# Row tiles of two blocks loaded into idle modulation buffers, and convolution taps kept behind the sums of squares of q and k

## The chip, the cores and the metric

The kernel runs on one core of one Trainium2 chip. The metric is the device time of one execution in microseconds (us). The engines are TensorE (PE, matmuls), VectorE (DVE), ScalarE (ACT), GpSimd (POOL) and SyncE (SP), whose queue issues nearly all DMAs. Each works through its own queue in order.

## The reference, cut to what matters

One layer of a streaming encoder, over 2048 prompt rows and 64 sample rows of width 1024, all in float32:

```python
mod = silu(c) @ w_ada + b_ada                      # six vectors: sh1, sc1, gt1, sh2, sc2, gt2
h = rms_norm(x, norm1_g) * (1 + sc1) + sh1
glu_a, glu_b, q, k, v, g_conv, g_attn = split(h @ w_in)
u = glu_a * sigmoid(glu_b)
conv = silu(layer_norm(depthwise_conv31(u) + b_dw)) @ w_conv_out
q, k = rms_norm(q, q_norm_g), rms_norm(k, k_norm_g)   # per head of 64
o = band_attention(q, k, v, rel_bias) @ w_attn_out
x = x + gt1 * ((sigmoid(g_conv) * conv + sigmoid(g_attn) * o) @ w_o)
h2 = rms_norm(x, norm2_g) * (1 + sc2) + sh2
gate, up = split(h2 @ w_ffn_in)
x = x + gt2 * ((silu(gate) * up) @ w_ffn_out)
```

The change lies in the first half, up to the mixers' outputs; the merge and the feed-forward part are untouched.

## The kernel before

**Blocks and stages.** The 2112 rows are cut into four blocks (`PBLOCKS`, b = 0 to 3; the text calls them blocks one to four): 576 rows, then three times 512. Each block goes through the stages of `ORDER`: q, the first quarter of the convolution channels (0), k, quarter 1, v, quarters 2 and 3, then g, the sixteen column groups of the two gates. Beside these products run the attention of the block, the convolution's taps and its norm, and, during the gates, the norm of the next block's rows. Matmul operands are split into a high and a low part, and each product takes three matmuls. This first half of the kernel ends near 1200 us.

**What sets the order.** The program is written out by Python in one pass. A model of the engines' loads (`Stream`, line 170) decides when the side jobs (`Lane`, line 108) emit their next piece: when PE's modelled time has passed what they yielded. DMA times are not modelled; a load counts as landed a fixed time after it was written (`X_LAG`, 8000 ns of modelled PE time, for row tiles). After that a scheduler lays out each engine's queue, by its own model of the times. It may move an instruction ahead of earlier ones that it believes are not ready. `tc.issue_after(ins)` keeps the instructions of its block behind `ins` on the same engine. Nothing is reordered at run time.

**Rows of the next block.** `load_ahead` (line 1129) takes the next tile of 128 rows from `to_load` and loads it into a buffer with the tag "x" of the pool `wa`, which has three. Stores of v (`store_v`, line 1021) and a few k rows of block one use the same tag. At gate group `NORM_G` (11) of a block, the main loop (line 1616) calls `load_ahead` three times. `norm_tile` (line 1135) then squares the rows on ACT (`square`), takes the power -1/2 of the mean on POOL (`rsqrt_mean`, line 722), scales the rows on DVE, turns them on PE in two groups of four 128x128 pieces (tile `pt`), and makes `hh` and `hl`. With its second group it calls `load_ahead` for one more tile. At most two tiles are in work at a time. `hh` and `hl` are still read by the gates of the block before; `free["columns"]` tells how far they are done with.

**Modulation.** Six products of `c` with `w_ada` are made from slabs of 512 KB (`Slabs`, line 230), which are loaded into four buffers of 4 KB per partition with the tag "wmod". `fill` (line 239) loads the next slab as soon as one is given back. The first sixteen slabs (keys of five parts) are used while block one's rows are prepared; the other 32 are used in blocks two and three, four behind each of the stages 0 to 3 (`MODS`). So the four buffers hold the next four slabs from block one's start to block two's stage 0.

**Taps.** `convolve` (line 1232) applies the 31 taps of a channel quarter, 30 of them one DVE operation each (`y<-u,wd,y`). They are emitted when DVE's modelled load allows, and each stays behind the last score traced so far (`scores`, filled in `softmax_max`, line 1347). In block one's k stage there are no scores yet.

**q and k.** `qk_rows` (line 1032) takes the product of one tile from PSUM: ACT makes squares (`sq`) and a copy (`kn`), DVE sums the squares per head (`ssq<-sq`) and makes the mean (`t<-ssq`), POOL the power (`r<-t,mhalf`), DVE the scaled rows (`kn<-kn,r`), PE turns them (`pt<-ident,kn`), ACT and DVE split them (`part_h`, `part_l`), and SP stores them.

Of the kernel before, what the change touches and what calls it, by code (L numbers as in the profile page):

```python
# [16 lines left out]
P = 128  # L17
# [15 lines left out]
QB = 512  # L33

PBLOCKS = [(0, 576), (576, 1088), (1088, 1600), (1600, 2112)]
# [11 lines left out]
X_LAG = 8000.0  # L47
# [182 lines left out]
class Slabs:  # L230
# [3 lines left out]
    def __init__(self, sync, other, pool, stream, keys, source, held):  # L234
        self.sync, self.other, self.pool, self.stream = sync, other, pool, stream
        self.keys, self.source, self.held = keys, source, held
        self.ready, self.used, self.given, self.freed = [], 0, 0, 0

    def fill(self):
        while len(self.ready) < min(len(self.keys), self.freed + self.held):  # L240
            (src,), a, b = self.source(self.keys[len(self.ready)])
            w = self.pool.tile([P, a, b], F32, tag="wmod", name="wmod", bufs=self.held)
            i = len(self.ready)
            (self.other if i < self.held and i % 2 else self.sync).dma_start(w, src)
            self.ready.append(w)

    def get(self, key):
        assert self.keys[self.used] == key
        self.used += 1
        while len(self.ready) < self.used:  # L250
            self.free(self.freed + 1)
        return self.ready[self.used - 1]

    def done(self):
        self.given += 1
# [356 lines left out]
def streaming_layer(ctx: ExitStack, tc: tile.TileContext, I, O):  # L612
    nc = tc.nc
    stream = Stream()
# [383 lines left out]
            dve.memset(bias[r : r + HD, c : c + HD], BIG)  # L998


    def store_kq(src, n, dst, col, g=None):

        pt = ps_g.tile([P, 4, P], F32, tag="gp", name="pt")
        for hp in range(4):
            pe.transpose(pt[:, hp, :n], src[:n, hp * P : (hp + 1) * P], ident[:n, :n])
        stream.after("act", "pe")
        hi, lo = parts(shape=(P, 4, P))
        if g is None:
            split(hi[:, :, :n], lo[:, :, :n], pt[:, :, :n])
        else:  # L1010
            act.activation(hi[:, :, :n], pt[:, :, :n], AF.Copy, scale=g)
            stream.after("dve", "act")
            dve.scalar_tensor_tensor(lo[:, :, :n], pt[:, :, :n], g, hi[:, :, :n].bitcast(F32), ALU.mult, ALU.subtract)

        def store():
            for j, t in enumerate((hi, lo)):
                nc.sync.dma_start(dst[j, :, :, col : col + n].rearrange("h p t -> p h t"), t[:, :, :n].bitcast(F32))

        stream.at(stream.when("act", "dve"), store)
# [12 lines left out]
    def qk_rows(ps, n, g, dst, col, out_rows, spare=False):  # L1032
        sq = temp("sq", (P, NH, HD))
        ssq = wk.tile([P, NH], F32, tag="ssq8", bufs=5)
        if spare:
            kn = wa.tile([P, 2, NH, HD], F32, tag="x", name="kn", bufs=3)[:, 0]
        else:
            kn = wa.tile([P, NH, HD], F32, tag="kn", bufs=3)
        pv = ps[:n].rearrange("p (h d) -> p h d", h=NH)
        stream.after("act", "pe")  # L1040
        act.activation(sq[:n], pv, AF.Square)
        act.activation(kn[:n], pv, AF.Copy)
        yield stream.when("act")
        dve.tensor_reduce(ssq[:n], sq[:n], AX.X, ALU.add)
        r = rsqrt_mean(wk, ssq[:n], n, NH, HD)
        yield stream.when("pool")
        e, name = either(512, TT_LESS)
        e.tensor_tensor(kn[:n], kn[:n], r.unsqueeze(2).to_broadcast([n, NH, HD]), ALU.mult)
        t = stream.when(name)
        if out_rows is not None:  # L1050
            ko = temp("ko", (P, NH, HD))
            e, name = either(512, TT_LESS)
            e.tensor_tensor(ko[:n], kn[:n], gk[:n].unsqueeze(1).to_broadcast([n, NH, HD]), ALU.mult)
            stream.at(stream.when(name), lambda: nc.sync.dma_start(out_rows, ko[:n].rearrange("p h d -> p (h d)")))
        yield t + KN_LAG
        store_kq(kn.rearrange("p h d -> p (h d)"), n, dst, col, g)
# [70 lines left out]
    ahead_x, to_load = {}, []  # L1127

    def load_ahead():

        if to_load:
            t = to_load.pop(0)
            ahead_x[t] = load_x(t, P, wa, "x", 3), stream.load["pe"] + X_LAG

    def norm_tile(lo, t, free):

        c = slice(t - lo, t - lo + P)
        while t not in ahead_x:
            load_ahead()
        x_t, landed = ahead_x.pop(t)  # L1140
        yield landed
        r = square(x_t, P)
        yield stream.when("pool")
        dve.tensor_scalar(x_t, x_t, r, None, ALU.mult)
        yield stream.when("dve") + PE_LAG
        for g in range(2):
            pt = ps_g.tile([P, 4, P], F32, tag="gp", name="pt")
            h = temp("h32", (P, 4, P))
            for k in range(4):
                pe.transpose(pt[:, k], x_t[:, (4 * g + k) * P : (4 * g + k + 1) * P], ident)  # L1150
            if g:
                stream.at(stream.when("pe"), load_ahead, True)
            stream.after("dve", "pe")
            for k in range(4):
                kk = 4 * g + k
                dve.tensor_scalar(h[:, k], pt[:, k], A1[:, kk, 0:1], B1[:, kk, 0:1], ALU.mult, ALU.add)
            yield stream.when("dve")
            yield lambda: free["columns"] >= c.stop
            f = slice(4 * g, 4 * g + 4)
            act.activation(hh[:, f, c], h, AF.Copy)  # L1160
            yield stream.when("act")
            dve.tensor_tensor(hl[:, f, c], h, hh[:, f, c].bitcast(F32), ALU.subtract)
# [35 lines left out]
    def kts(t, a=0, b=KT):  # L1198
        return [t[:, k] for k in range(a, b)]


    scores = []
    UW = HIST + QB + HIST + SMP
    YW = UW - HIST

# [26 lines left out]
    def convolve(u, y, ct, b):  # L1232
        w = UW if b == 0 else HIST + QB
        n = w - HIST
        states = [(cs_s, HIST + SMP)] if b == 0 else [(cs_p, w)] if b == len(PBLOCKS) - 1 else []
        if states:
            yield stream.when("dve") + TURN_LAG
        for rows_, e in states:
            pt = ps_g.tile([P, 512], F32, tag="gp", name="pt")
            pe.transpose(pt[:HIST, :P], u[:, e - HIST : e], ident)  # L1240
            s = wa.tile([HIST, P], F32, tag="cc", name="cc", bufs=2)
            dve.tensor_scalar(s, pt[:HIST, :P], 0.5, None, ALU.mult)
            stream.at(stream.when("dve"), lambda s=s, rows_=rows_: nc.sync.dma_start(rows_[:, ct * P : (ct + 1) * P], s))
            yield
        gps.tensor_copy(hist[:, ct], u[:, w - HIST : w])
        dve.tensor_scalar(y[:, ct, :n], u[:, :n], wd[:, ct, 0:1], bdw[:, ct : ct + 1], ALU.mult, ALU.add)
        for k in range(1, TAPS):
            with tc.issue_after(scores[-1]) if scores else nullcontext():
                dve.scalar_tensor_tensor(
                    y[:, ct, :n], u[:, k : k + n], wd[:, ct, k : k + 1], y[:, ct, :n], ALU.mult, ALU.add  # L1250
                )
            yield
# [94 lines left out]
    def softmax_max(ps, n, w, bias):  # L1347
        pr = wk.tile([P, 640], F32, tag="pr", name="pr", bufs=8)
        sm = wk.tile([P, 4], F32, tag="sm", name="sm", bufs=9)
        nb = ps.shape[1]  # L1350
        stream.after("dve", "pe")

        dve.tensor_tensor_reduce(
            out=pr[:n, :w].rearrange("p (a b) -> p a b", a=nb), in0=ps, in1=bias.rearrange("p (a b) -> p a b", a=nb),
            scale=-0.125, scalar=3e38, op0=ALU.add, op1=ALU.min, accum_out=sm[:n, 0:1],
        )
        scores.append(dve.last.ins)
        free = stream.when("dve")
        stream.after("act", "dve")
        act.activation(pr[:n, :w], pr[:n, :w], AF.Exp, bias=sm[:n, 0:1], scale=-1.0, accum_out=sm[:n, 2:3])  # L1360
        return pr, sm, free, stream.when("act")
# [230 lines left out]
    for b, stage in ORDER:  # L1592
        lo, hi = PBLOCKS[b]
# [20 lines left out]
        elif stage == "g":  # L1614
            for g in gates(b, free):
                if g == NORM_G:
                    to_load += list(ahead)
                    for _ in range(3):
                        load_ahead()
                    for gen in ahead.values():  # L1620
                        norm_lane.add(gen)
                if g == SIDE_G and b == len(PBLOCKS) - 1:
                    work.drain()
                    conv.drain()
                    stream.flush()
                    side.close()
                    wc = ctx.enter_context(tc.tile_pool(name="wc", bufs=1, side="right"))
                    cs = tile_chunks(*CBLOCKS[0])[0]
                    src = load_mixed(*cs, 0)
                    first_gates = gate_columns(*cs, 0)  # L1630
# [621 lines left out]
```

## Time and profile before

| what | us |
|---|---|
| median of 3 runs | 2994.62 |
| lowest and highest | 2992.54 and 2999.41 |
| the profiled execution | 2994.99 |
| its span, first to last instruction | 2993.2 |
| PE busy in it | 2912.7 |
| DVE busy in it | 2024.7 |
| PE busy in its first 1200 us | 1144.05 |
| PE busy in the other 1793.2 us | 1768.63 |

A row of a timeline gives the start on the span's clock, the length, the engine (a q behind its name means its queue, which issues a DMA), the line, the operation and what it writes and reads, and in brackets how long the engine had been idle and what ended that. Most instructions carry L102, the line of the helper that records them, so they are told apart by their tiles. A row of a table of stretches gives the busy time of each engine in it, the clock that was granted to TensorE (1.00 is full), the mean share of time that the DMA engines worked, and what they moved.

### The profile page before, as it was taken

The numbers are of one execution on the slowest core, as the hardware profiler recorded it, in microseconds if no ns is written. First come the engines' busy times: TensorE is split into PE (matmuls) and PEld (weight loads), VectorE is DVE, ScalarE is ACT, GpSimd is POOL, SyncE is SP. The second block draws the span as 40 slices with busy tenths as digits, with TensorE's granted clock in tenths as the row PEclk, the third lists the DMA queues.
The fourth block names the chain that finished last, engine by engine and source line by source line (L and its number), as shares of the span: only waits on it lengthen the run. The fifth ranks groups of instructions, "written<-read, shape, count | busy, mean of one in ns | idle before, by whom it ended". The sixth has DMA issues, their size and how long they took to land.

```text
span 2993.2 us, 44914 instructions
## 1 busy us (share of the span) xinstructions
PE 2912.7 (97%) x16259; PEld 2593.7 (87%) x16259; DVE 2024.7 (68%) x3596; ACT 1355.1 (45%) x2437; POOL 1141.4 (38%) x734
## 2 busy tenths in 40 slices
PE   7999899999999999989999999999999999999999
PEld 4899777787888788888989889999999999999998
DVE  5887687767857885477677755666666657466666
ACT  3335643662456257464444335534444345344442
POOL 0201310111011102354566433256666741466667
PEclk9999999999999999999999999999999999999999
DMA  8889889888987789885444786423333975333333
GB/s 290 289 284 304 266 288 314 282 255 275 308 280 221 275 246 286 254 293 166 141 141 152 232 269 216 138 89 115 118 101 115 307 248 183 96 93 116 116 102 127
DMA packets 467724, 628.06 MB, mean 210 GB/s; under 512 B 36276, under 2 KB 314664, under 8 KB 467501
## 3 DMA queue, kind: packets, MB, share of 16 engines
q1 hardware_dynamic: 453456, 605.58, 62.5%
q10 hardware_dynamic: 14045, 19.60, 1.9%
q8 instruction: 128, 2.10, 0.3%
q14 instruction: 95, 0.78, 0.1%
HBM read 476.53 MB, written 148.54 MB: 209 GB/s over the span
## 4 chain that ended last, share of the span: by engine, by line
PE 80%; DVE 8%; DMA 4%; ACT 2%; POOL 2%; issue 2%; SPq 1%; ACTq 0%; DVEq 0%; POOLq 0%
PE ps L102 51%; PE pd L102 16%; PE pw L102 5%; DVE y L102 3%; PE sc L102 2%; PE po L102 2%; PE ptp L102 2%; DVE wlo L102 1%; PE pt L102 1%; PE pa L102 1%; ACT whi L102 1%; DMA tg<-g_d 1%; POOL r L102 1%; POOL wlo L102 1%; DVE pw L102 1%
## 5 line engine op out<-in xcount | busy, mean ns | idle before, releaser
L102 PE MATMUL ps<-t,whi 128*128 128x384 f32 (+1 forms) x2112 | 502.5, 322 | 8.8 <-ACT t L102 5.0
L102 POOL TENSOR_TENSOR wlo<-wst,whi 128x1024 fp32r<-128x1024 f32 (+1 forms) x157 | 358.4, 2292 | 287.1 <-ACT whi L102 251.6
L102 ACT ACTIVATE whi<-wst 128x1024 fp32r<-128x1024 f32 (+1 forms) x264 | 257.5, 978 | 331.9 <-PE ps L102 113.8
L102 PE MATMUL ps<-b,whi 128*128 128x384 f32 (+1 forms) x1584 | 381.3, 326 | 6.1 <-DVE early L102 3.3
L102 PEld LDWEIGHTS ps<-t,whi 128*128 128x128 f32 x2112 | 367.7, 188 | 15.8 <-ACT t L102 5.2
L102 DVE SCALAR_TENSOR_TENSOR y<-u,wd,y 128x512 f32<-128x512 f32 (+1 forms) x480 | 369.1, 773 | 6.8
L102 PE MATMUL ps<-hh,whi 128*128 128x512 f32 (+2 forms) x992 | 361.5, 364 | 0.0
L102 DVE TENSOR_TENSOR acc<-acc,pd 128x512 f32<-128x512 f32 (+1 forms) x464 | 311.6, 685 | 66.9 <-PE pd L102 64.1
L102 PE MATMUL ps<-hl,whi 128*128 128x512 f32 (+2 forms) x992 | 345.3, 348 | 0.0
L102 PE MATMUL ps<-hh,wlo 128*128 128x512 f32 (+2 forms) x992 | 345.1, 348 | 0.0
L102 PE MATMUL ps<-t,wlo 128*128 128x384 f32 (+1 forms) x1056 | 339.2, 321 | 0.7 <-POOL wlo L102 0.7
L102 PE MATMUL pd<-whi,hid 128*128 128x512 f32 (+1 forms) x1016 | 325.2, 391 | 0.5 <-DVE acc L102 0.5
L102 PEld LDWEIGHTS ps<-b,whi 128*128 128x128 f32 x1584 | 278.6, 189 | 12.0 <-DVE early L102 4.2
L102 POOL TENSOR_TENSOR r<-t,mhalf 128x1 f32<-128x1 f32 (+3 forms) x68 | 84.1, 1239 | 453.2 <-DVE t L102 448.0
L102 PE MATMUL ps<-b,wlo 128*128 128x384 f32 (+1 forms) x792 | 256.9, 325 | 0.0
L102 ACT ACTIVATE pr<-pr,sm 128x640 f32<-128x640 f32 (+3 forms) x272 | 200.3, 747 | 102.8 <-DVE sm L102 100.5
L102 PEld LDWEIGHTS pd<-whi,hid 128*128 128x128 f32 (+1 forms) x1016 | 185.9, 183 | 45.2 <-DVE acc L102 0.9
L102 PEld LDWEIGHTS ps<-hh,wlo 128*128 128x128 f32 x992 | 186.6, 188 | 21.8
L102 PEld LDWEIGHTS ps<-hh,whi 128*128 128x128 f32 x992 | 187.2, 189 | 18.5 <-issue 1.6
L102 PEld LDWEIGHTS ps<-hl,whi 128*128 128x128 f32 x992 | 187.3, 189 | 15.4 <-issue 1.4
L102 PEld LDWEIGHTS ps<-t,wlo 128*128 128x128 f32 x1056 | 198.2, 188 | 1.9 <-POOL wlo L102 1.3
L102 PE MATMUL pd<-wlo,hid 128*128 128x512 f32 (+1 forms) x508 | 198.5, 391 | 0.0
(225 smaller groups left out, 6173.5 us busy)
## 6 DMA issues: line engine op xcount, KB each, us to landing
whi<-w_din_h SPq DMA_DIRECT2D x72, 512.0 KB, 6.7
wlo<-w_din_l SPq DMA_DIRECT2D x72, 512.0 KB, 7.5
wst<-sum_d SPq DMA_DIRECT2D x132, 256.0 KB, 2.7
wfo<-in_w_ffn_out SPq DMA_DIRECT2D x64, 512.0 KB, 3.3
wmod<-in_w_ada SPq DMA_DIRECT2D x46, 512.0 KB, 7.3
sum_d<-ws SPq DMA_DIRECT2D x88, 256.0 KB, 2.9
wst<-in_w_ffn_in SPq DMA_DIRECT2D x84, 256.0 KB, 3.1
wst<-in_w_in SPq DMA_DIRECT2D x40, 512.0 KB, 9.4
```

What stands on the lines that cost most here:

```text
L102: self.last = f(*args, **kw)
```

## The change

`Slabs` gets a limit `open`: at first only the sixteen slabs of the first modulation may be loaded, and `open_all` lifts it. `norm_tile` calls `open_all` behind the second group of turnings of a block's last tile; for other tiles it calls `load_ahead` as before. `load_ahead` puts the tiles of block three into "x" as before, and those of blocks two and four into "wmod". At `NORM_G` blocks one and three load all four tiles of the next block at once, block two three. The list `scores` becomes `ahead_of_taps`, and the mean that follows each sum of squares of q and k is entered too, so that each tap stays behind the last score or mean traced so far.

```diff
@@ class Slabs
+        self.open = sum(len(key) == 5 for key in keys)
+
     def fill(self):
-        while len(self.ready) < min(len(self.keys), self.freed + self.held):
+        while len(self.ready) < min(self.open, self.freed + self.held):
...
+    def open_all(self):
+        if self.open < len(self.keys):
+            self.open = len(self.keys)
+            self.fill()
@@ qk_rows
         dve.tensor_reduce(ssq[:n], sq[:n], AX.X, ALU.add)
         r = rsqrt_mean(wk, ssq[:n], n, NH, HD)
+        ahead_of_taps.append(dve.last.ins)
@@ load_ahead
             t = to_load.pop(0)
-            ahead_x[t] = load_x(t, P, wa, "x", 3), stream.load["pe"] + X_LAG
+
+            place = ("x", 3) if PBLOCKS[2][0] <= t < PBLOCKS[2][1] else ("wmod", 4)
+            ahead_x[t] = load_x(t, P, wa, *place), stream.load["pe"] + X_LAG
@@ norm_tile
             if g:
-                stream.at(stream.when("pe"), load_ahead, True)
+                stream.at(stream.when("pe"), M.open_all if t + P == lo + QB else load_ahead, True)
@@ convolve
-            with tc.issue_after(scores[-1]) if scores else nullcontext():
+            with tc.issue_after(ahead_of_taps[-1]) if ahead_of_taps else nullcontext():
                 dve.scalar_tensor_tensor(
@@ softmax_max
-        scores.append(dve.last.ins)
+        ahead_of_taps.append(dve.last.ins)
@@ main loop, stage g
                     to_load += list(ahead)
-                    for _ in range(3):
+                    for _ in range(3 if b == 1 else 4):
                         load_ahead()
```

More of the change, by code (lines that the diff above doesn't have):

```diff
@@ L998, in bias_rows @@
             dve.memset(bias[r : r + HD, c : c + HD], BIG)
+    ahead_of_taps = []
     def store_kq(src, n, dst, col, g=None):
@@ L1199, in kts @@
         return [t[:, k] for k in range(a, b)]
-    scores = []
     UW = HIST + QB + HIST + SMP
```

## The prediction

> **What bounds the kernel now.** I read the page of the profile first, for the engine that ends last, then the waits of that engine, then the stretches around its longest waits, engine by engine.
>
> ```profile
> PE 2912.7 (97%) x16259; PEld 2593.7 (87%) x16259; DVE 2024.7 (68%) x3596; ACT 1355.1 (45%) x2437; POOL 1141.4 (38%) x734
> ```
>
> TensorE (PE) is busy for 97% of the span. The change touches no matmul, so all that it can win or lose is idle time of PE, and time in which PE runs at a lower granted clock. The waits of PE (total in us, times, longest) say which idle time is within its reach:
>
> ```profile
> PE pt L102 <- DVE x_t L102: 10.9, 6, 5.7
> PE sc L102 <- DVE sm L102: 7.9, 7, 2.4
> ...
> PE pt L102 <- DVE kn L102: 3.5, 2, 2.3
> ```
>
> Half of the first row is one wait of 5.7 us for a scaled tile of x rows. The third is about rows of q and k. Here is the stretch of the 5.7 us, from the timelines of SyncE's queue (SPq), ScalarE (ACT), GpSimd (POOL), VectorE (DVE) and PE; columns are start, length, what, and in brackets the idle time ahead of it:
>
> ```profile
> 299.12 3.24 SPq L1116 DMA_DIRECT2D x_t<-in_x_prompt  x3
> ...
> 342.98 1.25 SPq L1116 DMA_DIRECT2D x_t<-in_x_prompt  x1
> ...
> 353.33 0.61 ACT L102 ACTIVATE junk<-x_t 128x512 f32<-128x512 f32 x1
> ...
> 343.43 0.55 POOL L102 TENSOR_TENSOR r<-t,mhalf 128x1 f32<-128x1 f32 x1
> ...
> 344.02 0.75 DVE L102 TENSOR_SCALAR x_t<-x_t,r 128x1024 f32<-128x1024 f32 x1 [4.91 <-POOL r L102]
> ...
> 355.90 0.76 DVE L102 TENSOR_SCALAR x_t<-x_t,r 128x1024 f32<-128x1024 f32 x1 [0.23 <-POOL r L102]
> ...
> 356.80 1.09 PE L102 MATMUL pt<-ident,x_t 128*128 128x128 f32 x4 [5.66 <-DVE x_t L102]
> ```
>
> Three tiles of block two's rows are loaded at 299 us, the fourth only at 342.98, when the first has given its buffer back. Its squares start at 353.33, it is scaled at 355.90, and PE, idle since 356.80 - 5.66 = 351.14, turns it at 356.80. The third tile, loaded 43 us earlier, was scaled at 344.02. What the wait does to the clock stands in the table of 4 us stretches (length; busy time of PE, PEld, DVE, ACT, POOL; then granted clock, DMA share, GB/s):
>
> ```profile
> 350.00:354.00 4.00, 1.04 (x5) 0.30 (x3) 1.30 (x6) 3.11 (x9) 0.00 (x0) 0.84 1.07 337
> 354.00:358.00 4.00, 1.09 (x4) 0.72 (x4) 3.08 (x10) 3.29 (x8) 0.56 (x1) 0.50 1.04 356
> 358.00:362.00 4.00, 3.99 (x10) 3.08 (x11) 4.00 (x12) 2.35 (x5) 2.62 (x1) 0.50 0.80 188
> 362.00:366.00 4.00, 4.00 (x22) 3.30 (x21) 4.00 (x9) 1.93 (x4) 0.21 (x1) 0.88 0.29 110
> ...
> 378.00:382.00 4.00, 4.00 (x21) 3.10 (x19) 2.41 (x5) 0.96 (x2) 1.63 (x1) 1.00 1.02 396
> ```
>
> A mean of 0.88 in the fourth row means 0.96 us of it at half clock, so the half clock ends near 362.96; by the first row it began near 352.72.
>
> **The change, part by part.**
>
> *Four row tiles at once.* For blocks two and four the fourth load moves to the other three, at about 302.4 us. The four buffers are idle there, and the extra issue takes SyncE about 1.1 us (3.24 / 3). The fourth tile can then follow the third: its power behind the third's (343.43 + 0.55), its scaling behind the third's (344.77), ready near 346, five us ahead of 351.14. The wait goes: -5.66. With PE busy throughout, I expect the clock to stay up: the 6.16 us from 356.80 to 362.96 at half clock become 3.08. Together **-8.74**. Block four gains nothing: the view of PE's waits has no wait for x_t once block two's rows are turned. The third tile's own short wait stays, since it is for the power on POOL (the 4.91 us on DVE), not for a load.
>
> The Trainium skill ("TensorE: Matmul & The Clock Gate", Terms) prices the penalty as throttled time times (1 - K/N). For 10.24 us at half clock that is an estimate of 5.1 us, and the sum would be 2.0 us better; but the rows show PE idle for the first part of it, and idle time is counted already.
>
> *Modulation slabs later.* The four slabs that fill those buffers now move behind the turning of block two's last tile. What they meet there:
>
> ```profile
> 57.61 4.71 SPq L244 DMA_DIRECT2D wmod<-in_w_ada  x4
> ...
> 363.28 0.49 PE L102 MATMUL pt<-ident,x_t 128*128 128x128 f32 x3
> ...
> 368.70 0.33 SPq L466 DMA_DIRECT2D whi<-w_din_h  x1
> ...
> 381.20 0.47 PE L102 MATMUL ps<-hh,whi 128*128 128x512 f32 x1
> ...
> 388.77 1.93 PE L102 MATMUL pa<-wmod,cl 128*32 128x256 f32 x32
> ...
> wlo<-w_din_l SPq DMA_DIRECT2D x72, 512.0 KB, 7.5
> ```
>
> At 57.61 nothing is gained: PE waits for no DMA between there and block one's k products. Their new place is the second turning of block two's last tile, at 363.28 - 8.74 = 354.5 on the shortened time; they are first read at 388.77 - 8.74 = 380.0. Four slabs are 2.1 MB, 5.3 us at the 396 GB/s of the last stretch above, so even with some microseconds of issue they land near 363, 17 us early. But SyncE issues in order, and behind them stands the second weight of the convolution's first stage: issued at 368.70, used at 381.20, 12.5 us between. Both ends move up alike; 5.3 us of slabs in front leave 7.2, and the page's median from issue to landing is 7.5. I take a loss of **+0.3**. Bounds: 0 (the stretches at 362 to 370 had DMA to spare) and 5.3 with up to 3.1 of lost clock behind it, 8.4.
>
> *Taps behind the sums.* In block one's k stage the rows are:
>
> ```profile
> 103.39 7.04 DVE L102 SCALAR_TENSOR_TENSOR y<-u,wd,y 128x606 f32<-128x606 f32 x8
> 110.34 0.67 DVE L102 TENSOR_REDUCE ssq<-sq 64x8 f32<-64x512 f32 x1
> ...
> 117.14 0.83 DVE L102 SCALAR_TENSOR_TENSOR y<-u,wd,y 128x606 f32<-128x606 f32 x1
> 117.90 0.16 DVE L102 TENSOR_SCALAR t<-ssq 128x8 f32<-128x8 f32 x1
> ...
> 101.95 0.58 ACT L102 ACTIVATE kn<-ps 64x512 f32<-64x512 f32 x1
> 115.48 0.47 ACT L102 ACTIVATE part_h<-pt,gqk 128x256 fp32r<-128x256 f32 x1 [12.95 <-PE pt L102]
> ...
> 118.20 1.65 POOL L102 TENSOR_TENSOR r<-t,mhalf 128x8 f32<-128x8 f32 x1 [4.05 <-DVE t L102]
> ...
> 115.01 0.43 PE L102 MATMUL pt<-ident,kn 64*128 64x64 f32 x4 [2.26 <-DVE kn L102]
> ...
> 120.72 0.63 PE L102 MATMUL pt<-ident,kn 128*128 128x128 f32 x4 [0.94 <-DVE t L102]
> ```
>
> ACT has the squares ready at 102; eight taps keep the sum from DVE until 110.34, and PE waits 2.26 us for the rows at the end. Without them the sum starts near 103.4, 7 us sooner, and this wait goes. The tile behind it has one tap between sum and mean (117.14 to 117.90; the mean is the t row): 0.76 of its 0.94 goes. What the taps lose they take later, beside matmuls. Block three has the same picture:
>
> ```profile
> 711.27 0.59 ACT L102 ACTIVATE kn<-ps 128x512 f32<-128x512 f32 x1
> ...
> 717.25 0.68 DVE L102 TENSOR_REDUCE ssq<-sq 128x8 f32<-128x512 f32 x1
> ...
> 718.81 2.05 POOL L102 TENSOR_TENSOR r<-t,mhalf 128x8 f32<-128x8 f32 x1 [5.89 <-DVE t L102]
> ...
> 721.74 0.63 PE L102 MATMUL pt<-ident,kn 128*128 128x128 f32 x4 [1.23 <-DVE kn L102]
> ```
>
> The sum comes over 5 us after its squares, the wait is 1.23. Together **-2.26 - 0.76 - 1.23 = -4.25**; bounds 0, if the taps stay where they are, and -4.43. One guard is loosened: a tap behind a sum no longer waits for a score traced before it. A tap in front of a score costs up to 0.8 us, seven times at most by the sc row (5.6 in all); I take 0, since a score that is ready still goes first.
>
> Against this part speaks a rule of the Trainium skill ("SBUF — State Buffer", SBUF: two separate sides): a DVE operation with two SBUF inputs and a GpSimd operation lock each other out. The rows fit: the power took 1.65 us with no tap beside it and 2.05 with one. Taps that are freed just as the mean is out would sit beside each power, and the second wait would shrink by 0.36 in place of 0.76, the sum being 0.4 worse.
>
> Sum: -8.74 + 0.3 - 4.25 = -12.7. The profiled execution took 2994.99 us (its span 2993.2 and 1.8 around it), 0.4 above the median of 2994.62. **2994.99 - 12.7 = 2982.3.**
>
> **The rivals.**
>
> *The taps do not move* (they were traced ahead of the sums and keep their place). For it: DVE's order is settled when the program is laid out, not by arrival. Against: in both blocks above the sum came several microseconds behind its squares, so taps passed it that could have waited. 2994.99 - 8.74 + 0.3 = 2986.6.
>
> *More than counted is won.* In block four, v's last weight is late:
>
> ```profile
> 999.68 0.63 SPq L466 DMA_DIRECT2D whi<-w_dqkv_h  x1
> ...
> 1006.83 0.50 PE L102 MATMUL ps<-whi,hh 128*128 128x512 f32 x1 [2.01 <-DMA whi<-w_dqkv_h]
> ```
>
> It is issued behind a store of k rows, which waits for DVE. Sums that come earlier bring that store forward. -2.0 and, by the ratio of the first stall, 1.1 of clock: 2979.2.
>
> *The slabs give the gain back.* The upper bound above, 8.4 for 0.3, makes 2990.4: within 0.2%. For it: DMA is at 1.0 or more from 374 us on. Against: the pocket at 362 to 370.
>
> *Slower: the taps arrive late at the convolution's norm.* In block one a tap behind a sum waits for ACT, which stands from 102.5 to 115.48, so DVE idles where it ran nine taps (7.04 + 0.83 = 7.9 us). From 230 us DVE is full and PE waits at the norm's sums:
>
> ```profile
> 210.00:220.00 10.00, 6.12 (x12) 1.00 0.80 262
> ...
> 260.00:270.00 10.00, 10.00 (x18) 1.00 0.92 308
> ...
> 272.37 0.43 PE L102 MATMUL pm<-s,ones 128*128 128x64 f32 x2 [2.64 <-POOL s L102]
> ```
>
> If the 7.9 us arrive there, the 2.64 grow by as much, and by some 3.1 of clock: 11.0. Twice that, with block three, is 22.0: 2994.99 - 12.7 + 22.0 = 3004.3. It decides from 12.7 us of delay at those sums. Against it: 3.9 us idle at 210 to 220 alone, where the taps can catch up.
>
> **How the numbers follow.** Forecast 0.36, taps unmoved 0.15, more won 0.12, slabs late 0.20, norm late 0.17. About 0.2%, or 6 us, is what a measurement of this kernel can tell from no change; so faster 0.63, same 0.20, slower 0.17. The range runs from 2975 (all the bounds of the gain, and a little more for waits that shift) to 3000, which holds the late slabs and leaves out the late norm.
>
> **What would show it.** Right: four x loads together near 300 us; no wait over 2 us before block two's last tile; clock 1.00 from 350 to 366; the four slabs issued near 355 and landed before 380; in the k stages each sum within 1 us of its squares; no wait for kn over 0.3 us. Wrong: PE waits for wmod or whi between 360 and 400, a norm's sum that waits over 5 us, or new waits of sc for sm. The forecast rests most on PE not meeting another late thing when it comes 8.7 us sooner to 351 us and what follows.

## The result, and the profile after

| | us |
|---|---|
| before, median of 20 runs | 2995.29 (2988.83 to 3004.89) |
| after, median of 20 runs | 2999.97 (2995.10 to 3004.45) |
| ratio after / before | 1.0016, 95% interval 1.0010 to 1.0022 |
| profiled execution of after, and its span | 3002.77, 3000.7 |

2982.3 was forecast. The kernel became 4.7 us slower and stands at the very upper end of the range. The two profiled executions are 7.8 us apart, 3 more than the medians, so what the traces show below does not add up to the 4.7 exactly. The page's row of TensorE and the waits of TensorE in the changed kernel (total in us, times, longest) answer to the first rows of the prediction:

```profile
PE 2919.7 (97%) x16259; PEld 2595.2 (86%) x16259; DVE 2026.4 (68%) x3596; ACT 1354.9 (45%) x2437; POOL 1142.3 (38%) x734
```

```profile
PE sc L102 <- DVE sm L102: 14.2, 16, 1.9
...
PE pt L102 <- DVE x_t L102: 4.3, 4, 1.4
...
PE pt L102 <- DVE kn L102: 1.6, 2, 1.2
```

The two rows that the change aimed at shrank as forecast: x_t from 10.9 to 4.3, kn from 3.5 to 1.6. But the wait of scores (sc) for the scores' DVE step (sm) went from 7.9 us in 7 waits to 14.2 in 16, and PE is counted busy for 7.0 us longer (2919.7 against 2912.7) with the same 16259 matmuls. The stretch that the forecast was about went well (length; busy PE, PEld, DVE, ACT, POOL; granted clock, DMA share, GB/s):

```profile
350.00:354.00 4.00, 4.00 (x23) 3.38 (x22) 4.00 (x14) 4.00 (x10) 0.00 (x0) 1.00 0.70 174
354.00:358.00 4.00, 4.00 (x23) 3.29 (x22) 3.79 (x11) 3.26 (x8) 2.42 (x1) 1.00 0.84 233
358.00:362.00 4.00, 4.00 (x23) 3.30 (x22) 3.90 (x10) 2.78 (x7) 0.00 (x0) 1.00 0.43 110
```

Here PE had stood for 5.66 us and run at half clock; now it is full at clock 1.00. The same matmul in both traces, counted among the products that read `whi` and `hh`, shows how long that lasted:

| product matmul | before, us | after, us | difference |
|---|---|---|---|
| 501st | 331.8 | 327.1 | -4.7 |
| 526th | 364.5 | 354.2 | -10.3 |
| 576th | 411.0 | 407.0 | -4.0 |
| 601st | 439.3 | 441.9 | +2.6 |
| 1001st | 812.4 | 819.2 | +6.8 |

At 354 us the changed kernel was 10.3 us ahead. Between 354 and 442 us (the 526th to the 601st product) it lost 12.9. PE's timeline there, first the seventh head of block one (start, length, what, and in brackets the idle time ahead of it):

```profile
370.87 0.42 PE L102 MATMUL sc<-kk,q 128*128 128x128 f32 x2
372.11 0.50 PE L102 MATMUL sc<-kk,q 128*128 128x256 f32 x2 [0.83 <-DVE sm L102]
373.14 0.62 PE L102 MATMUL sc<-kk,q 128*128 128x384 f32 x2 [0.53 <-DVE sm L102]
374.41 0.73 PE L102 MATMUL sc<-kk,q 128*128 128x512 f32 x2 [0.66 <-DVE sm L102]
375.93 0.51 PE L102 MATMUL sc<-kk 128*64 128x320 f32 x2 [0.79 <-DVE sm L102]
```

and the eighth:

```profile
424.02 0.50 PE L102 MATMUL sc<-kk,q 128*128 128x256 f32 x2 [1.93 <-DVE sm L102]
425.04 1.01 PE L102 MATMUL sc<-kk,q 128*128 128x384 f32 x2 [0.52 <-DVE sm L102]
426.71 1.22 PE L102 MATMUL sc<-kk,q 128*128 128x512 f32 x2 [0.66 <-DVE sm L102]
428.72 0.80 PE L102 MATMUL sc<-kk 128*64 128x320 f32 x2 [0.79 <-DVE sm L102]
```

The five scores of a head follow each other with no product between (the first of head eight, at 420.55, is followed by six matmuls of an attention output, `po`, and no product). The program gives them two banks of PSUM, the memory that matmuls write, in turn; a score can start only when DVE's step on an earlier score has read its bank out, and PE stands until then. In the kernel before, all scores of the two heads have products between them, and only head eight's second waits, for 2.40 us. Its row, then the start of head seven:

```profile
425.08 0.50 PE L102 MATMUL sc<-kk,q 128*128 128x256 f32 x2 [2.40 <-DVE sm L102]
```

```profile
387.53 0.33 PE L102 MATMUL sc<-kk,q 128*128 128x128 f32 x2
387.70 0.45 PE L102 MATMUL ps<-hh,whi 128*128 128x512 f32 x1
387.98 0.39 PE L102 MATMUL ps<-hl,whi 128*128 128x512 f32 x1
388.21 0.39 PE L102 MATMUL ps<-hh,wlo 128*128 128x512 f32 x1
388.44 0.40 PE L102 MATMUL sc<-kk,q 128*128 128x256 f32 x2
```

Behind the eighth head's scores the clock falls. The stretches of after, then of before:

```profile
420.00:424.00 4.00, 1.59 (x10) 1.11 (x8) 2.43 (x7) 0.82 (x3) 2.06 (x1) 1.00 0.65 167
424.00:428.00 4.00, 2.73 (x6) 1.30 (x6) 2.50 (x9) 2.71 (x8) 0.00 (x0) 0.57 0.95 323
428.00:432.00 4.00, 3.28 (x13) 2.94 (x14) 3.41 (x10) 3.13 (x7) 0.21 (x1) 0.50 1.05 367
432.00:436.00 4.00, 4.00 (x16) 3.16 (x14) 0.00 (x0) 0.76 (x2) 0.00 (x0) 0.65 1.03 420
```

```profile
420.00:424.00 4.00, 2.68 (x13) 1.89 (x12) 2.03 (x5) 0.26 (x2) 1.76 (x2) 1.00 1.00 329
424.00:428.00 4.00, 2.92 (x14) 2.44 (x15) 3.90 (x12) 2.01 (x6) 0.00 (x0) 1.00 1.00 326
```

The kernel before idles there for 1.32 + 1.08 = 2.4 us, the one wait of head eight, and keeps its clock. After idles 2.41 + 1.27 + 0.72 = 4.4 and has a clock of 0.57, 0.50 and 0.65 for 12 us.

So the theory for the experiments, **A: the layout of TensorE's queue changed with the row loads, the scores of two heads came to stand together, and their waits and the clock behind them ate the gain.** Rivals: **B**, the taps' loosened guard makes scores wait; **C**, the held-back slabs cost it; **D**, raised by the fourth run, that pinning the scores is worth its gain in any version.

### The profile page after: what moved, and what is told of

It reads as the page before. It is cut to its first block, busy times and chain, and to the rows that moved or that the text cites. A ratio compares the mean times of both kernels' runs of the same rounds, so it can differ in the third digit from the quotient of the medians.

```text
span 3000.7 us, 44900 instructions
## 1 busy us (share of the span) xinstructions
PE 2919.7 (97%) x16259; PEld 2595.2 (86%) x16259; DVE 2026.4 (68%) x3596; ACT 1354.9 (45%) x2437; POOL 1142.3 (38%) x734
## 4 chain that ended last, share of the span: by engine, by line
PE 79%; DVE 8%; DMA 6%; ACT 2%; POOL 2%; issue 2%; SPq 1%; ACTq 0%; DVEq 0%; POOLq 0%
PE ps L102 50%; PE pd L102 15%; PE pw L102 6%; DVE y L102 3%; PE sc L102 2%; PE po L102 2%; PE ptp L102 2%; DVE wlo L102 2%; PE pt L102 1%; PE pa L102 1%; DMA tg<-g_d 1%; ACT whi L102 1%; POOL r L102 1%; DVE pw L102 1%; POOL wlo L102 1%
```

## The experiments

All times are medians beside runs of the kernel before on the same chip; differences below are (ratio - 1) x 2995.

| run | ratio to before, 95% interval | us |
|---|---|---|
| after | 1.0016 (1.0010 to 1.0022) | +4.8 |
| e1 rows and slabs | 1.0033 (1.0021 to 1.0045) | +9.9 |
| e2 taps | 1.0001 (0.9992 to 1.0010) | +0.3 |
| e3 slabs | 1.0008 (0.9999 to 1.0016) | +2.4 |
| e4 after, scores pinned | 0.9969 (0.9957 to 0.9981) | -9.3 |
| e5 before, scores pinned | 0.9993 (0.9983 to 1.0003) | -2.1 |
| e6 before, scores together | 1.0041 (1.0028 to 1.0054) | +12.3 |
| e7 rows and slabs, pinned | 0.9992 (0.9984 to 1.0000) | -2.4 |
| e8 after, head seven pinned | 0.9986 (0.9978 to 0.9995) | -4.2 |
| e9 e4, head eight 10 us later | 0.9975 (0.9966 to 0.9984) | -7.5 |
| e10 e4, head eight 14 us later | 0.9982 (0.9973 to 0.9990) | -5.4 |
| e11 block four's rows | 0.9999 (0.9990 to 1.0008) | -0.3 |
| e12 after, both guards | 1.0008 (1.0000 to 1.0017) | +2.4 |
| e13 taps, pinned | 0.9987 (0.9977 to 0.9997) | -3.9 |
| e14 taps and slabs, pinned | 0.9987 (0.9978 to 0.9996) | -3.9 |
| e15 e4, one slab held back | 0.9996 (0.9987 to 1.0005) | -1.2 |

### One part at a time

Rows and slabs alone (e1): the change without

```diff
@@ qk_rows
-        ahead_of_taps.append(dve.last.ins)
```

> The row loads and held-back slabs alone; taps guarded by the last score as before. Theory A (the new order of TensorE's queue comes with the row loads: block one's heads seven and eight are scored in one piece, five scores with no product between, and lose by waits for sm and half clock what the x_t wait gave): no 5.7 us wait for x_t, but waits of sc for sm of 0.5 to 2 us in two bunches near 372 and 425 and a half clock behind them; 2997 to 3001 us, within 2 us of the changed kernel. Rival B (the taps' loosened guard costs it): the x_t gain stays, 2985 to 2989.

3004.08 us, above the range expected. Head seven's scores stand together here too (the last two rows):

```profile
186.37 0.66 PE L102 MATMUL sc<-kk,q 128*128 128x128 f32 x2 [3.07 <-DMA kk<-k_d]
...
374.22 0.42 PE L102 MATMUL sc<-kk,q 128*128 128x128 f32 x2
375.46 0.51 PE L102 MATMUL sc<-kk,q 128*128 128x256 f32 x2 [0.83 <-DVE sm L102]
```

B falls: the loss is there with the old guard, and is even larger. The first row is a wait that no theory had: block one's first score waits 3.07 us for its k rows. With the taps behind the sums (after) it does not: the same score starts at 184.03 with no wait.

Taps alone (e2), on the kernel before:

```diff
@@ qk_rows
+        ahead_of_taps.append(dve.last.ins)
@@ convolve
-            with tc.issue_after(scores[-1]) if scores else nullcontext():
+            with tc.issue_after(ahead_of_taps[-1]) if ahead_of_taps else nullcontext():
```

> The taps' guard alone; rows and slabs loaded as before. Theory A: TensorE's order in block two stays near the old one, so 2991 to 2996 us, with the kn wait of 2.26 us near 115 gone. Rival B (the loosened guard costs the gain): about 12 us over the forecast of this part alone, so 3000 to 3006 us.

2995.96 us: no loss, but no gain either.

Slabs alone (e3): e1 with the rows loaded as before the change,

```diff
-            place = ("x", 3) if PBLOCKS[2][0] <= t < PBLOCKS[2][1] else ("wmod", 4)
+            place = ("x", 3)
...
-                    for _ in range(3 if b == 1 else 4):
+                    for _ in range(3):
```

> Only the four slabs are held back until block two's last tile is turned; that tile is still loaded late and the taps are guarded as before. Rival C (slabs arriving late give the gain back): TensorE waits for wmod or a weight behind them between 375 and 400 us, 2998 to 3003 us. Theory A: the scores of head seven keep their old spacing in TensorE's queue, those of head eight come partly together; the 5.7 us wait stays; 2994 to 2998 us.

2997.99 us. PE waits for no slab between 375 and 400 us, and head seven's scores stand apart; only the last two of head eight's stand together. So head seven's bunch needs the row loads; the slabs alone do not make it. C falls as the cause of the loss in after. What e3 itself may lose (2.4 us, interval -0.3 to 4.8) goes with the same wait for k rows in block one as in e1 (4.19 us at 188.00), which after does not have.

### Scores pinned

```diff
-                    pe.matmul(ps[:n, 0, :w], q2[:, d, t : t + n], kk[:, :w], start=d == 0, stop=d == 1)
+                    mm = pe.matmul(ps[:n, 0, :w], q2[:, d, t : t + n], kk[:, :w], start=d == 0, stop=d == 1)
+                    if not d:
+                        tc.keep_in_program_order(mm)
```

Each score of block one now stays behind the matmul that was traced ahead of it, in the changed kernel (e4).

> The changed kernel, with each score of block one's heads pinned behind the matmul that was traced ahead of it, so that head seven's five scores stand apart again (3, 3, 6 and 51 products between them), head eight's only in part (3, 0, 0, 39). Theory A: the bunch near 372 goes with its 2.8 us of waits for sm, the one near 425 keeps two of its waits; 2990 to 2996 us, 4 to 9 below the changed kernel. If scores in one piece are not the cause: within 2 us of the changed kernel, 2998 to 3002.

2985.54 us, 14 us below the changed kernel (0.9969 against 1.0016; 10 to 18 by the two intervals), where Theory A had expected 4 to 9. Its timeline has head seven as the kernel before had it:

```profile
378.06 0.33 PE L102 MATMUL sc<-kk,q 128*128 128x128 f32 x2
378.23 0.45 PE L102 MATMUL ps<-hh,whi 128*128 128x512 f32 x1
378.51 0.39 PE L102 MATMUL ps<-hl,whi 128*128 128x512 f32 x1
378.74 0.39 PE L102 MATMUL ps<-hh,wlo 128*128 128x512 f32 x1
378.97 0.39 PE L102 MATMUL sc<-kk,q 128*128 128x256 f32 x2
```

The control (e5) is the same edit in the kernel before.

> Control: the kernel before with the same pins of the scores as in the fourth run. In it head seven's and head eight's scores stand apart already. Theory A (the pins only undo what the change did to TensorE's order): 2991 to 2997 us, within 4 us of the kernel before. Rival D (the pins are worth some 10 us in any version, and the change as such gains nothing): 2983 to 2988 us.

2992.71 us, no difference from before that its interval can tell. D falls: the pins are worth some 2 us by themselves, not 14.

The inverse (e6) takes the pause between the scores of heads seven and eight out of the kernel before:

```diff
-                yield free + PE_LAG, SCORE_ROOM
+                if x != 0 or h < 6:
+                    yield free + PE_LAG, SCORE_ROOM
```

> The inverse: the kernel before, with the scores of heads seven and eight of block one traced in one piece, so that they stand together in TensorE's queue (3, 0, 0, 9 and 41, 0, 0, 0 products between them). Loads and taps as before. Theory A: new waits of sc for sm of 0.5 to 0.9 us in two bunches, 2 to 3 us together, and with a half clock behind them up to 8 us: 2997 to 3004 us. If scores in one piece cost nothing: 2993 to 2997.

3006.00 us, 12.3 over before and more than expected. In the layout head seven's scores kept some products, so nearly all of it is head eight:

```profile
420.91 0.27 PE L102 MATMUL po<-ph,vv 128*128 128x64 f32 x1 [1.94 <-DMA vv<-v_d]
423.95 0.79 PE L102 MATMUL sc<-kk,q 128*128 128x256 f32 x2 [2.10 <-DVE sm L102]
426.55 1.01 PE L102 MATMUL sc<-kk,q 128*128 128x384 f32 x2 [1.81 <-DVE sm L102]
...
431.48 0.80 PE L102 MATMUL sc<-kk 128*64 128x320 f32 x2 [1.43 <-DVE sm L102]
```

```profile
420.00:430.00 10.00, 4.92 (x15) 2.78 (x15) 3.72 (x14) 4.66 (x13) 3.19 (x2) 0.64 0.76 225
430.00:440.00 10.00, 7.39 (x24) 5.48 (x24) 9.47 (x21) 4.74 (x11) 0.09 (x1) 0.51 0.74 302
```

Here PE idles 7.7 us in 20 and runs at 0.64 and 0.51. One of the waits is for v rows (1.94), which the traced order brought along, so the 12.3 are not all of the scores. With it, A is shown from both sides: taking head seven's bunch and a part of head eight's out of the changed kernel gives 14 us, putting one into the kernel before costs up to 12.

Head seven alone (e8), in the changed kernel:

```diff
-                    if not d:
+                    if not d and h == 6:
                         tc.keep_in_program_order(mm)
```

> The changed kernel with the pins on head seven of block one alone: its scores stand apart (3, 3, 6, 51 products between), head eight's stay together (3, 0, 0, 0). Theory A: the waits near 372 go (2.8 us), those near 425 stay with their half clock: 2990 to 2996 us, between the changed kernel and the run with all pins. If the second bunch's half clock was the whole loss: 2997 to 3000; if the first bunch was: 2984 to 2987.

2990.02 us: in between, as expected. The traces show where the time went. By the count of the table of products above, the way from the 526th product to the 601st takes:

| before | after | e4 | e8 | e6 |
|---|---|---|---|---|
| 74.7 us | 87.6 us | 78.0 us | 78.7 us | 90.4 us |

The pins on head seven alone shorten this stretch by 8.9 us, far more than the 2.8 us that its scores wait: at head eight, whose scores still stand together, PE idles 2.9 us in place of 4.4, and the half clock lasts 6.8 us in place of 10.2. The pins on the other heads add 0.7 us here. So 9.6 of the 14 us of e4 lie in this stretch, and for the rest the traces name no single place. What a bunch costs depends on what stands around it: head eight's makes e8 4.0 us longer than before from the 576th product to the 601st, and e6 13.8 us.

Head eight apart as well, on e4 (e9; e10 with 14000):

```diff
-        yield loaded[i]
+        yield loaded[i] + (10000.0 if x == 0 and h == 7 else 0.0)
```

> The changed kernel with all pins, and head eight's scores traced 10 us later by the program's own clock, so that they stand apart as well (3, 3, 6, 45 products between). Theory A: of the run with pins alone (2985.5) go the three waits of sc for sm near 418 (1.7 us) and the half clock behind them (some 1.7 us): 2981 to 2984 us, the time that was forecast for the change. If the rest of head eight's bunch costs nothing: 2984 to 2987.

> The same with 14 us, which puts 75 products ahead of head eight's first score and 6, 3, 3 and 48 between the others. Theory A: as in the run before, 2981 to 2984 us, or some tenths more where head eight's end comes late to block two's first head. If its delay is the dearer thing: over 2986.

2988.28 and 2991.13 us. Both missed: nothing more was won. The waits of e4 that were to go came back as others, in e9 as one wait for sm, in e10 as two for weights:

```profile
418.57 0.80 PE L102 MATMUL sc<-kk,q 128*128 128x256 f32 x2 [1.94 <-DVE sm L102]
```

```profile
416.41 0.76 PE L102 MATMUL ps<-hh,whi 128*128 128x512 f32 x1 [2.09 <-DMA whi<-w_din_h]
418.99 0.80 PE L102 MATMUL ps<-hh,wlo 128*128 128x512 f32 x1 [0.96 <-DMA wlo<-w_din_l]
```

### The terms of the sum, with the order kept

Rows and slabs with pins, without the taps (e7: the edits of e1 and e4):

> The row loads and slabs with the pinned scores, taps guarded by the last score as before: what the taps' part is worth in the pinned order. By the prediction's term the taps' part is worth 4.25 us, so 2989 to 2991 us against 2985.5 with it; by the runs without pins (3004.1 without it, 3000.0 with it) the same 4 us. If the taps' part only shifts waits: 2984 to 2987.

2992.17 us, a little above the range expected, so the taps' part is worth 6.9 us here (0.9992 against 0.9969; 3 to 11 by the two intervals). Taps with pins (e13: the edits of e2 and e4), and taps and held-back slabs with pins but the fourth tile loaded late (e14: those of e3 and e4, with the taps' guard as changed):

> Taps behind the sums plus the pinned scores, rows and slabs loaded as before: with the fourth run this prices the whole part of rows and slabs where the scores stand apart in both. By the profiles' stretches the early tile is worth some 4 us, not the 8.7 of the forecast, so 2988 to 2991 us. If the part is worth 8.7 net of the slabs: 2993 to 2996. If it is worth nothing even with pins, as the fifth and seventh run would have it without the taps (2992.7 and 2992.2): 2984 to 2987.

> The fourth run's kernel with block two's last tile (and block four's) loaded late again, as before the change, the slabs still held back: the wait of 5.7 us for x_t comes back and nothing else. The early load alone is then this run less the fourth. By the forecast 8.7 us: 2993 to 2996. By the profiles' stretches some 4 us: 2988 to 2991. The difference to the thirteenth run is what holding back the slabs costs: 0 to 2 us.

2991.38 and 2990.98 us, at one ratio, 0.9987: with taps and pins, holding back the slabs costs nothing that can be told. e14 less e4 is the early load alone: 0.0018, or 5.4 us (1 to 10 by the two intervals), where 8.7 was forecast. The traces do not show this gain where the wait is, as the next section says. The wait that it removes is smaller here than in the kernel before, as in every run with pinned scores and a late tile:

```profile
349.04 0.63 PE L102 MATMUL pt<-ident,x_t 128*128 128x128 f32 x4 [3.11 <-DVE x_t L102]
```

(3.26 us in e5, 3.48 in e13.) Three more: block four's loads alone, on the kernel before (e11); both guards in one, on the changed kernel (e12); and e4 with one slab held back in place of four (e15).

```diff
@@ e11
-            ahead_x[t] = load_x(t, P, wa, "x", 3), stream.load["pe"] + X_LAG
+            place = ("x", 3) if t < PBLOCKS[3][0] else ("wmod", 4)
+            ahead_x[t] = load_x(t, P, wa, *place), stream.load["pe"] + X_LAG
...
-                    for _ in range(3):
+                    for _ in range(4 if b == 2 else 3):
@@ e12, convolve
-            with tc.issue_after(ahead_of_taps[-1]) if ahead_of_taps else nullcontext():
+            with ExitStack() as held:
+                for ins in scores[-1:] + ahead_of_taps[-1:]:
+                    held.enter_context(tc.issue_after(ins))
@@ e12, softmax_max
-        ahead_of_taps.append(dve.last.ins)
+        scores.append(dve.last.ins)
@@ e15
-        self.open = sum(len(key) == 5 for key in keys)
+        self.open = sum(len(key) == 5 for key in keys) + 3
...
-            place = ("x", 3) if PBLOCKS[2][0] <= t < PBLOCKS[2][1] else ("wmod", 4)
+            place = ("x", 3) if t != PBLOCKS[1][1] - P else ("wmod", 4)
...
-                    for _ in range(3 if b == 1 else 4):
+                    for _ in range(3 if b else 4):
```

> The kernel before, with block four's four row tiles loaded together into the modulation's buffers (idle there for good); block two's loads, the slabs and the taps as before. By the prediction block four gains nothing: 2993 to 2997 us. TensorE's order hardly changes, so Theory A says the same. A gain or a loss of over 4 us would say that block four's loads matter.

> The changed kernel with each tap queued behind both the last score and the last mean that were traced ahead of it, so that the guard loosened by the change is whole again. By Theory A TensorE's order decides and stays the same: within 2 us of the changed kernel, 2998 to 3002. If taps that pass a score make TensorE wait for sm (the prediction's bound of 5.6 us, taken at 0): 2994 to 2996.

> The fourth run's kernel with only one slab held back: three of block two's tiles go to their old buffers, the fourth into the one buffer of the modulation that stays free, block four as before. If holding back four slabs costs something (a late score at 186 us, a first-stage weight behind them), this run is 1 to 3 us below the fourth: 2982 to 2985. If not, within 2 us of it: 2984 to 2988.

e11, 2995.70 us: block four gains nothing, as forecast. e12, 2998.07 us: within 2 us of the changed kernel's median and with the same bunches, so the loosened guard costs nothing that can be told from 0 (2.4 us by the ratios, -0.7 to 5.5). e15, 2993.55 us: it should have been at or below e4 and is 8 above. In its trace, one wait of 1.47 us for a first-stage weight at 421.13 is new; that explains a part at most. Its executions lie between 2987 and 2996 us, and the traced one is at 2988.0, as fast as the traced one of e4 (2988.35), so this trace may not show what costs it; it stays open.

## Why the prediction was wrong, point by point

**The step that failed** is the sentence "The change touches no matmul, so all that it can win or lose is idle time of PE, and time in which PE runs at a lower granted clock", read as if PE's order were given, so that the sum has no term for a new order, and with it the last one, "The forecast rests most on PE not meeting another late thing". The change touches no matmul, but it moved them: the scheduler lays out each queue by its own model of when data is ready, and a tile that is ready earlier moved the scores of block one's heads. From e4 against after, that order costs 14 us (10 to 18), more than the forecast sum of 12.7. "New waits of sc for sm" stood among the signs of a wrong forecast, and they came, but no rival had them as its mechanism, and they had no price in the sum. That the time still lies inside the range is luck: its upper end was meant for late slabs, and PE waits for no slab in block two. Why the model puts the scores together when the tile is early was not found out.

**Four row tiles at once, -8.74.** The wait of 5.66 us went, and the clock stayed at 1.00 from 350 to 362. But a part of the idle time only moved: a little earlier PE now waits for two scores of head six, which it did not in the kernel before, and the clock is at 0.58 from 342 to 346.

```profile
342.93 0.80 PE L102 MATMUL sc<-kk,q 128*128 128x256 f32 x2 [1.41 <-DVE sm L102]
346.78 0.62 PE L102 MATMUL sc<-kk,q 128*128 128x384 f32 x2 [0.53 <-DVE sm L102]
```

From the 501st product to the 526th PE took 32.7 us before and takes 27.1 after, of which it idles 7.6 and 3.8: 5.6 us won where 8.74 was forecast. With pinned scores the traces show no gain there: 28.5 us in e4, and 28.1 in e14, which loads the tile late. There e14 waits 3.11 us for x_t, and e4 waits 1.40 and 1.99 us for sm, the second in this row:

```profile
345.28 0.86 PE L102 MATMUL sc<-kk,q 128*128 128x384 f32 x2 [1.99 <-DVE sm L102]
```

So the 5.4 us between the medians of e14 and e4 are not the wait that the term was about, and what they are is not shown. The idle 5.66 us were partly a matter of order too, since pins alone leave 3.1 to 3.5 of them. "Four x loads together near 300 us" was wrong as well:

```profile
71.66 0.38 SPq L1127 DMA_DIRECT2D x_t<-in_x_prompt  x1
...
118.06 0.56 SPq L1127 DMA_DIRECT2D x_t<-in_x_prompt  x1
...
295.25 1.03 SPq L1127 DMA_DIRECT2D x_t<-in_x_prompt  x1
```

With a free buffer the scheduler issued three of them (one more at 74.49) in block one, up to 230 us ahead.

**Slabs later, +0.3.** Right in block two: issued at 359.34, and PE waits for none of them there. e13 and e14 stand at one ratio, each known to some 3 us, so the size cannot be told from 0. The reading that PE waits for no DMA behind 57.61 us overlooked a wait of 1.13 us for a slab that ends at 59.40; in after it is 2.48 us, so without the four slabs it did not shrink. And e1 and e3, without the taps' part, show a cost in block one that the step did not look for. There head one's pieces of q and k are issued later than in after:

```profile
180.22 3.22 SPq L1394 DMA_DIRECT2D kk<-k_d  x3
```

```profile
175.20 3.88 SPq L1395 DMA_DIRECT2D kk<-k_d  x3
```

5 us apart, with a 3.07 us wait in the first (e1) and none in the second (after).

**Taps behind the sums, -4.25.** In block one it did what was said: the squares end at 101.88 + 0.58, the sum starts at 102.76, 0.3 us behind them where it was 8 us late, and both waits for kn are gone. In block three it did not: squares at 717.42 + 0.60 = 718.02, sum at 723.89, and the wait is the old one:

```profile
717.42 0.60 ACT L102 ACTIVATE sq<-ps 128x512 f32<-128x512 f32 x1 [1.33 <-PE ps L102]
...
723.89 0.68 DVE L102 TENSOR_REDUCE ssq<-sq 128x8 f32<-128x512 f32 x1
...
728.38 0.63 PE L102 MATMUL pt<-ident,kn 128*128 128x128 f32 x4 [1.23 <-DVE kn L102]
```

A tap is held behind the last mean traced before it. Taps that were traced ahead of this sum are not, so by the program the rival "taps do not move" holds there. As a whole the part is worth 0.3 us of loss alone (e2, interval -2.4 to +3.0), 1.8 of gain with pins (e13 against e5, -2.4 to 6), and 5 to 7 beside the row loads (e1 against after, e7 against e4), where it also removes the wait for k rows of 3 us. A term measured by itself was not the term of the sum.

**The rivals.** The slabs gave nothing back. The norm of the convolution was not late: its waits fell from 6.2 to 4.9 us. In block four v's last weight came no earlier for PE: its wait grew to 2.6 (after) and 3.5 us (e4).

**The sum, once the order is kept**, is e4: -9.3 us (5.7 to 12.9) against the -12.7 that was forecast, at 2985.5 us the fastest version of this study. It ran five times; e9, e10 and e15, with the same pins and nearly the same loads, came out at -7.5, -5.4 and -1.2, so the true gain may be smaller.

## What to carry to other kernels

Where a scheduler lays out the queues, a change in when data arrives can change the order of every engine: compare the order of the bound engine's instructions before and after, ahead of any durations, and count a gain at the same instruction further on, since a wait that goes may come back as another. What is placed well only by the scheduler's guess, such as scores that need products between them, should be held there by an explicit order, or the gain of one stage pays for a bunch in another. And price two edits together as well as one by one: here the taps were worth nothing alone and 5 to 7 us beside the loads.

## What the runs showed of the hardware

Half clock came behind waits that are each short. In the changed kernel the longest idle time of PE between 420 and 430 us is the 1.93 us above; yet with 1.59 us busy in 4 the clock fell to half within the next 4 us, and PE, mostly busy again, stayed below full clock until the stretch after 436. The Trainium skill ("TensorE: Matmul & The Clock Gate", HAM oscillation — how this bites in real kernels) gives the rule that no idle gap should exceed about 3.4 us. The trace does not agree with it as a rule that is enough: no gap here was near 3.4, and what went with the half clock was several waits close together. By contrast, the kernel before idled 2.4 us in the 8 us from 420, in one piece, and kept 1.00. Where a wait falls in time may decide as well: in the changed kernel three spells of half clock begin at 342.68, 424.60 and 489.45 us and last 3.41, 10.24 and 3.41 us, and both the lengths and the distances between the starts are whole multiples of 3.41 us. No run here separates the two.
